# A hybrid decoder block on one core: twelve columns of w_in as split products, both halves of w_out in one wide PSUM tile, mixer outputs normalised ahead of it

## The chip, the cores and the metric

The kernel runs on one core of a Trainium2 chip. The time is what one execution takes on the device, in microseconds; three executions of the kernel before took 1172.45 (the median), 1170.61 and 1172.55 us. All rows below are from one profiled execution of it, which took 1174.26 us; its profiled span is 1172.4 us. Engines: PE multiplies matrices, DVE and POOL do elementwise work, ACT elementwise work with tables (and copies), SP issues most transfers.

## The reference

One layer over 256 positions of width 2048. The mixers take x through w_in (24 columns of 128 channels: 8 for the RG-LRU's input u, 8 for its gate, 8 for the S5 group), each group's result is normalised by itself, and w_out adds it to x; then a gated convolutional FFN of width 6144 follows.

```python
xn = rmsnorm(x, norm1_g[l])
proj = xn @ w_in[l]                       # 2048 -> 3072
rg_u, rg_gate, s5_u = proj[..., :D_RG], proj[..., D_RG:2 * D_RG], proj[..., 2 * D_RG:]
y_rg = rg_lru_group(rg_u, rg_gate, ...)   # conv, gates, linear scan, times gelu(gate)
y_s5 = s5_group(s5_u, ...)                # complex scan over 64 states, out = z * sigmoid(z @ w_glu + b_glu)
mixed = jnp.concatenate([rmsnorm(y_rg, out_norm_rg_g[l]),
                         rmsnorm(y_s5, out_norm_s5_g[l])], axis=-1)
x = x + mixed @ w_out[l]
x = x + conv_gated_mlp(rmsnorm(x, norm2_g[l]), ffn_w_up[l], ffn_conv_w[l], ffn_conv_b[l], ffn_w_down[l])
return rmsnorm(x, final_norm_g)
```

## The kernel before

Activations lie transposed, channels on the 128 partitions and the 256 positions (T) along the row. Weights come as tiles of 128 columns by 8 blocks of 128 rows (512 KB, tile `raw`, four in flight, issued by SP in the order of the program).

There are two kinds of product. `product_whole` (L185) multiplies the raw fp32 weights with fp32 activations, one matmul of 256 columns a block; each shows as two records in the trace. `product` (L170) splits: ACT copies the weights to a high part `wh` (`part`, L150), DVE subtracts it to get the low part `wl` (L151), and the activations have been split in the same way by `split` (high half by ACT, low half by DVE, L202 or L208). A `step` then sums high times high, high times low and low times high: narrow, in three matmuls of 256 columns (L158 to L160), or wide, in one matmul of 512 columns over both halves of the activations (L156) and one of 256 (L160). The wide form leaves two partial sums in PSUM which somebody has to add. Before, only the FFN is wide (`WIDE = "FD"`).

The 24 columns of w_in: four (0, 1, 16, 2) are done in the head while x arrives; the other 20 go through `product_whole`. Weight parts `wh` and `wl` have three buffers each, PSUM has four for products (tag "main") and one each for the small ones of the S5 mixer ("tp", "y", "bu").

The mixers and w_out are written as steps, called in the order of the string `ORDER` (a letter and an index). A scheduler then places the instructions on their engines by its own model of time; on each engine they run in the placed order. The letters: U, P, B and G are the RG-LRU (column of u with its convolution; gates; for four columns at once the decay a4 and the input b4, `rg_batch`; scan and gelu gate, `rg_out`). S, T, K, N, Y and F are the S5 group: its column; tables of sine and cosine, on POOL; matrices, on POOL, with four transposes on PE (L545) whose input `ball` POOL makes (L527), and small matmuls `cb` (L551); N the scan, whose matmuls `bu` (L572) feed a chain on DVE (L577 to L589) that ends in `wx`; Y the matmuls out of `wx` (L599 to L607); gelu. Z splits the S5 results and L multiplies with w_glu, applies the sigmoid and the gate (`s5_glu`). R and Q compute the two groups' 1/rms (`rstd`: a sum by PE, a root by ACT, a reciprocal by DVE, a broadcast by PE, a copy by ACT).

w_out takes one product of 8 blocks for each half of its rows and each of 16 output columns: W the upper half, from the unnormalised RG result. E multiplies W's sum by the group's 1/rms (DVE, L727) and adds it to x (POOL, L728); x is loaded again with the first E. V is the lower half, whose sum DVE multiplies by the other 1/rms and adds to x (L745, L746), then squares and splits for the FFN. That the norm comes after the product is why W and V can't share one PSUM sum.

The stages in the trace: head to 35 us; mixers to 232; W, L, V to about 355; FFN to 1160; final norm.

Of the kernel before, what the change touches and what calls it, by code (L numbers as in the profile page):

```python
# [8 lines left out]
F32 = mybir.dt.float32  # L9
# [5 lines left out]
P = 128  # L15
D = 2048
# [60 lines left out]
def block_kernel(ctx, tc, a, out):  # L77
# [204 lines left out]
    with ExitStack() as ph:
# [387 lines left out]
        def rg_batch(g):  # L670
# [13 lines left out]
            V.tensor_scalar(a4, q4, -2.0, -1.0, ALU.mult, ALU.add)  # L684
            G.tensor_tensor(b4, b4, q4, ALU.mult)
            G.tensor_tensor(b4, b4, tau, ALU.mult)

        def rg_out(j):
# [7 lines left out]
            fn(ge, u, AF.Gelu_apprx_tanh)  # L696
            yv = work.tile([P, T], F32, tag="rg", name="yv")
            V.scalar_tensor_tensor(yv, ge, -1.0, bj, ALU.mult, ALU.mult)
            add_sq(acc_rg, yv, j == 0)
            yr[j] = split(mix, f"y{j}", yv, col("grg", j))  # L700

# [17 lines left out]
        def rg_add(o):  # L719
            if not xr:  # L720
                for i in range(4):
                    t = keep(f"xq{i}", (P, 4, T))
                    nc.sync.dma_start(t, a["xT"][:, 4 * i:4 * i + 4, :])
                    xr.extend(t[:, k, :] for k in range(4))
                    xq2.append(t)
            u = work.tile([P, T], F32, tag="u", name="u")
            V.tensor_tensor(u, total(tops[o], "W" in WIDE), rs["rg"], ALU.mult)  # L727
            G.tensor_tensor(xr[o], xr[o], u, ALU.add)  # L728

        def s5_glu(j):  # L730
            ps = total(product(a["w_glu"], j, (0,), zs, "L" in WIDE), "L" in WIDE)
            sg = work.tile([P, T], F32, tag="cv", name="sg")
            fn(sg, ps, AF.Sigmoid, bias=col("bglu", j))
            ov = work.tile([P, T], F32, tag="rg", name="ov")
# [3 lines left out]
            tag, n = (("wa", WB), ("wb", WB), ("wx", WB), ("bt", WB))[j % 4]  # L738
            ys[j] = split(mw, tag, ov, col("gs5", j), bufs=n)

        def s5_top(o):

            ps = total(product(a["w_out"], o, (1,), ys, "V" in WIDE), "V" in WIDE)
            u = work.tile([P, T], F32, tag="u", name="u")
            V.tensor_tensor(u, ps, rs["s5"], ALU.mult)  # L745
            V.tensor_tensor(xr[o], xr[o], u, ALU.add)  # L746
            add_sq(acc2, xr[o], o == 0)
            x2[o] = split(cpool, f"x{o}", xr[o], col("g2", o))
# [153 lines left out]
```

## Time and profile before

| | before |
|---|---|
| median of three runs | 1172.45 us (1170.61 to 1172.55) |
| the profiled execution | 1174.26 us, span 1172.4 us |
| PE busy | 1145.3 us (98%), mean granted clock 0.988 |
| DVE, ACT, POOL busy | 805.4, 574.3, 209.7 us |

The page gives each engine's busy time, the span in 40 slices of 29.3 us with the busy share in tenths, and the clock granted to PE. A timeline has one row for each run of like instructions: start, time, engine, line, output and inputs, shapes, their count, and in brackets the idle time of the engine ahead with what ended it. Views by line give the count, the sum and the mean of one. PE's records overlap: a step's price is the distance of starts, not the time of a record.

### The profile page before, as it was taken

How to read it: one execution, taken by the hardware profiler on the slowest of the kernel's cores; microseconds unless marked ns; L12 is line 12 of the kernel's file. 1: busy time of each engine (PE TensorE's matmuls, PEld its weight loads, DVE VectorE, ACT ScalarE, POOL GpSimd, SP SyncE). 2: the span in 40 equal slices, each digit the busy share in tenths (PEclk: the TensorE clock that was granted, in tenths of full speed). 3: DMA queues.
4: the chain of work that ended last, by engine and by line, in shares of the span. 5: the costliest groups of instructions: out<-in, count | busy, mean ns of one | idle time of the engine just before them, and what ended most of it. 6: DMA issues, size and time to landing. Idle time of an engine off the chain costs nothing.

```text
span 1172.4 us, 19286 instructions
## 1 busy us (share of the span) xinstructions
PE 1145.3 (98%) x7454; PEld 1014.7 (87%) x7454; DVE 805.4 (69%) x1246; ACT 574.3 (49%) x897; POOL 209.7 (18%) x270
## 2 busy tenths in 40 slices
PE   9998979999999999999999999999999999999996
PEld 8787868889998888888888888888888888888886
DVE  7677564567797777878778787778777444444443
ACT  4342522255466555555555555555555444444432
POOL 5897665124231000000000000000000000000000
PEclk9998989999999999999999999999999999999998
DMA  7434435545566656666656666666656665665662
GB/s 274 139 110 152 134 123 155 170 148 181 180 187 184 187 194 183 195 189 189 195 185 195 186 192 188 190 191 188 193 185 194 183 187 188 183 189 184 186 190 92
DMA packets 65980, 209.27 MB, mean 178 GB/s; under 512 B 11872, under 2 KB 15584, under 8 KB 65888
## 3 DMA queue, kind: packets, MB, share of 16 engines
q1 hardware_dynamic: 65744, 207.97, 56.9%
q8 instruction: 58, 0.95, 0.3%
q14 instruction: 34, 0.28, 0.1%
q10 hardware_dynamic: 144, 0.07, 0.0%
HBM read 204.87 MB, written 2.10 MB: 177 GB/s over the span
## 4 chain that ended last, share of the span: by engine, by line
PE 88%; DVE 4%; POOL 4%; DMA 1%; issue 1%; ACT 1%; SPq 0%; DVEq 0%; ACTq 0%; POOLq 0%
PE ps L156 44%; PE ps L160 27%; PE ps L193 6%; PE ps L159 4%; PE ps L158 4%; PE ps L304 2%; PE y L602 1%; PE y L607 1%; POOL m L525 1%; DMA xq<-in_xT 0%; POOL cp L538 0%; DVE wa L584 0%; POOL m L526 0%; DVE xq L806 0%; POOL tm L506 0%
## 5 line engine op out<-in xcount | busy, mean ns | idle before, releaser
L156 PE MATMUL ps<-sp,wh 128*128 128x512 f32 x2256 | 787.1, 393 | 0.0
L160 PE MATMUL ps<-sp,wl 128*128 128x256 f32 x2624 | 738.0, 281 | 0.0
L151 DVE TENSOR_TENSOR wl<-raw,wh 128x1024 fp32r<-128x1024 f32 x328 | 403.8, 1231 | 245.1 <-ACT wh L150 243.7
L150 ACT CAST wh<-raw 128x1024 fp32r<-128x1024 f32 x328 | 344.8, 1051 | 429.2 <-PE ps L156 251.8
L156 PEld LDWEIGHTS ps<-sp,wh 128*128 128x128 f32 x2256 | 422.6, 187 | 95.6
L160 PEld LDWEIGHTS ps<-sp,wl 128*128 128x128 f32 x2624 | 496.6, 189 | 0.0
L245 POOL TENSOR_TENSOR accx<-accx,sq 128x256 f32<-128x256 f32 x29 | 34.9, 1203 | 800.6 <-ACT sq L244 800.6
L193 PE MATMUL ps<-xg,raw 128*128 128x256 f32 x640 | 146.5, 385 | 0.0
L193 PEld LDWEIGHTS ps<-xg,raw 128*128 128x128 f32 x640 | 121.1, 192 | 17.5 <-issue 0.3
L158 PE MATMUL ps<-sp,wh 128*128 128x256 f32 x368 | 104.6, 285 | 1.9 <-DVE u L727 1.9
L159 PE MATMUL ps<-sp,wh 128*128 128x256 f32 x368 | 104.8, 285 | 0.1
L777 DVE SCALAR_TENSOR_TENSOR cv<-u,par,cv 128x255 f32<-128x255 f32 x192 | 92.3, 480 | 4.1 <-ACT cv L775 0.7
L158 PEld LDWEIGHTS ps<-sp,wh 128*128 128x128 f32 x368 | 71.0, 193 | 2.2 <-DVE u L727 2.0
L159 PEld LDWEIGHTS ps<-sp,wh 128*128 128x128 f32 x368 | 71.1, 193 | 0.4 <-DVE sp L208 0.3
L775 ACT ACTIVATE cv<-u,par 128x256 f32<-128x256 f32 x96 | 57.2, 596 | 0.8 <-DVE u L773 0.8
L773 DVE TENSOR_TENSOR u<-t,rstd 128x256 f32<-128x256 f32 x96 | 40.4, 421 | 1.6
L167 DVE TENSOR_TENSOR t<-t,ps 128x256 f32<-128x256 f32 x96 | 39.7, 414 | 0.0
L166 ACT COPY t<-ps 128x256 f32<-128x256 f32 x96 | 34.7, 361 | 0.0
L304 PE MATMUL ps<-xg,raw 128*128 128x256 f32 x128 | 28.7, 384 | 0.2 <-ACT xg L279 0.2
L304 PEld LDWEIGHTS ps<-xg,raw 128*128 128x128 f32 x128 | 24.5, 193 | 4.0 <-ACT xg L279 0.6
L795 DVE TENSOR_TENSOR xq<-xq,ps 128x256 f32<-128x256 f32 x31 | 13.0, 421 | 16.4 <-PE ps L160 15.9
L538 POOL TENSOR_TENSOR cp<-m,m 64x192 f32<-64x192 f32 x32 | 20.7, 647 | 8.5 <-PE y L607 6.6
(231 smaller groups left out, 697.8 us busy)
## 6 DMA issues: line engine op xcount, KB each, us to landing
raw<-in_w_up SPq DMA_DIRECT2D x192, 512.0 KB, 3.5
raw<-in_w_down SPq DMA_DIRECT2D x96, 512.0 KB, 4.3
raw<-in_w_in SPq DMA_DIRECT2D x47, 512.0 KB, 3.8
raw<-in_w_out SPq DMA_DIRECT2D x32, 512.0 KB, 4.3
raw<-in_w_glu SPq DMA_DIRECT2D x8, 512.0 KB, 3.6
xq<-in_xT SPq DMA_DIRECT2D x7, 512.0 KB, 4.3
out_y<-xq SPq DMA_DIRECT2D x6, 256.0 KB, 2.1
rw<-in_rgw SPq DMA_DIRECT2D x8, 128.0 KB, 3.5
```

What stands on the lines that cost most here:

```text
L150: S.copy(wh, raw)
L151: V.tensor_tensor(wl, raw, wh.bitcast(F32), ALU.subtract)
L156: PE.matmul(ps, lhsT=wh[:, kk, :], rhs=x, start=first, stop=False)
L158: PE.matmul(ps[:, 0, :], lhsT=wh[:, kk, :], rhs=x[:, 0, :], start=first, stop=False)
L159: PE.matmul(ps[:, 0, :], lhsT=wh[:, kk, :], rhs=x[:, 1, :], start=False, stop=False)
L160: PE.matmul(ps[:, 0, :], lhsT=wl[:, kk, :], rhs=x[:, 0, :], start=False, stop=last)
L167: V.tensor_tensor(t, t, ps[:, 0, :], ALU.add)
L193: PE.matmul(ps, lhsT=raw[:, kk, :], rhs=x[j], start=j == 0, stop=j == n - 1)
L304: PE.matmul(ps, lhsT=raw0[i][:, k % KC, :], rhs=xs[k], start=k == 0, stop=k == KX - 1)
L773: V.tensor_tensor(u, ps, rs["n2"], ALU.mult)
L775: S.activation(cv, u, AF.Identity, bias=col("fcb", o), scale=col("fcw", 2 * 2 * KF + o))
L777: V.scalar_tensor_tensor(cv[:, d:], u[:, :T - d], col("fcw", (2 - d) * 2 * KF + o), cv[:, d:], ALU.mult, ALU.add)
```

## The change

Six things change.

1. `WHOLE` names the 12 columns of w_in that stay fp32. The other 12 (U7, S5, S6, S7 and the eight gates) become narrow split products. Their activations are split by the new step A0 (`x_split`), 16 high and 16 low halves in tiles of their own.
2. W and V are wide and go into the same PSUM tile: W opens the sum (`last=False`), V closes it (`first=False`), and DVE adds the two parts to x straight out of PSUM. E is gone, and L is always narrow, as it was.
3. For that the mixer results are normalised first: the new steps H and I (`normed`) multiply by the group's 1/rms on DVE and split. x is loaded again by D0.
4. In `rg_batch` the two products of b4 move from POOL to DVE.
5. The gate's results (`ov`, and the RG result) are written in place of tensors that are done with, no longer into a work tile.
6. `ORDER` is rewritten: Y comes after the next column's N, the S5 steps run further ahead of the columns, all L stand together before W, and V alternates with W from V0 on.

The diff, cut:

```diff
-W0 Z0 Z1 E0 W1 Z2 Z3 E1 W2 Z4 Z5 E2 W3 Z6 Z7 E3 L0 L1 W4 E4 L2 L3 W5 E5 L4 L5 W6 E6 L6 L7 W7 E7 W8 E8 W9 E9 Q0 W10
+Z0 Z1 Z2 Z3 Z4 Z5 Z6 Z7 L0 R0 L1 L2 H0 H1 L3 H2 H3 L4 H4 H5 L5 H6 H7 L6 L7 Q0 W0 W1 W2
+I0 I1 I2 I3 I4 I5 I6 I7 D0 V0 W3 V1 W4 V2 W5 V3 W6 V4 W7 V5 W8 V6 W9 V7 W10 V8 W11 V9 W12 V10 W13 V11 W14 V12 W15
...
+WHOLE = (0, 1, 16, 2, 3, 17, 4, 18, 5, 19, 6, 20)
...
-    WIDE = "FD"
+    WIDE = "FDV"
...
+    def products(ps, src, ot, kcs, xs, wide, first=True, last=True):
...
-                step(ps, wide, wh, wl, kk, xs[j], j == 0, j == n - 1)
+                step(ps, wide, wh, wl, kk, xs[j], first and j == 0, last and j == n - 1)
...
+        def x_split(k):
+            xp.append(split(cpool, f"x{k}", xs[k], None))
+
         def w_in_col(o):
-            return early[o] if o in early else product_whole(a["w_in"], o, (0, 1), xs)
+            if o in early:
+                return early[o]
+            if o in WHOLE:
+                return product_whole(a["w_in"], o, (0, 1), xs)
+            return product(a["w_in"], o, (0, 1), xp)[:, 0, :]
...
-            G.tensor_tensor(b4, b4, q4, ALU.mult)
-            G.tensor_tensor(b4, b4, tau, ALU.mult)
+            V.tensor_tensor(b4, b4, q4, ALU.mult)
+            V.tensor_tensor(b4, b4, tau, ALU.mult)
...
+        def normed(pool, tag, v, r, gcol, **kw):
+            V.tensor_tensor(v, v, r, ALU.mult)
+            return split(pool, tag, v, gcol, **kw)
...
         def rg_top(o):
-            tops[o] = product(a["w_out"], o, (0,), yr, "W" in WIDE)
+            tops[o] = psm.tile([P, 2, T], F32, tag="main", name="ps")
+            products(tops[o], a["w_out"], o, (0,), yr, "V" in WIDE, last=False)
...
-            u = work.tile([P, T], F32, tag="u", name="u")
-            V.tensor_tensor(u, total(tops[o], "W" in WIDE), rs["rg"], ALU.mult)
-            G.tensor_tensor(xr[o], xr[o], u, ALU.add)
...
         def s5_top(o):
-            ps = total(product(a["w_out"], o, (1,), ys, "V" in WIDE), "V" in WIDE)
-            u = work.tile([P, T], F32, tag="u", name="u")
-            V.tensor_tensor(u, ps, rs["s5"], ALU.mult)
-            V.tensor_tensor(xr[o], xr[o], u, ALU.add)
+            products(tops[o], a["w_out"], o, (1,), ys, "V" in WIDE, first=False)
+            flush()
+            for h in range(1 + ("V" in WIDE)):
+                V.tensor_tensor(xr[o], xr[o], tops[o][:, h, :], ALU.add)
```

Three places show what moves. In these rows stand the line, the operation, the output and inputs, the tile's size and a count; lines of the changed kernel are some 3 to 30 higher. The first place is PE between the `cb` matmuls of K0 and those of K1 (`tp` are K1's transposes, `pg` the RG gates). Before:

```order
L551 MATMUL cb<-cp_383,bp_382 32x96 x8
L572 MATMUL bu<-u_520,bt 64x64 x16
L193 MATMUL ps<-xg,raw 128x256 x5
L545 MATMUL tp<-par,ball 128x128 x2
L193 MATMUL ps<-xg,raw 128x256 x3
L545 MATMUL tp<-par,ball 128x128 x2
L193 MATMUL ps<-xg,raw 128x256 x11
```

And in the changed kernel:

```order
L561 MATMUL cb<-cp_383,bp_382 32x96 x8
L582 MATMUL bu<-u_520,bt 64x64 x2
L682 MATMUL pg<-rcv,rw 128x256 x2
L582 MATMUL bu<-u_520,bt 64x64 x14
L555 MATMUL tp<-par,ball 128x128 x4
L200 MATMUL ps<-xg,raw 128x256 x13
```

The eight matmuls of a column that stood between `bu` and the last transposes now stand behind them.

The second place is DVE in the chain of one N late in the mixers, N5 (from `bu` to the last `wx`). Before:

```order
L577 TENSOR_TENSOR wa_1770<-bu_1753,cs_t_1595 128x2x2x128
L577 TENSOR_TENSOR wb_1771<-bu_1753,sn_t_1594 128x2x2x128
L580 TENSOR_TENSOR wa_1770<-wa_1770,wb_1771 128x256
L581 TENSOR_TENSOR wa_1770<-wa_1770,wb_1771 128x256
L584 SCALAR_TENSOR_TENSOR wa_1770<-dec1_393,wa_1770 128x256 x2
L586 TENSOR_TENSOR wx_1772<-wa_1770,cs_t_1595 128x512
L586 TENSOR_TENSOR wb_1771<-wa_1770,sn_t_1594 128x512
L588 TENSOR_TENSOR wx_1772<-wx_1772,wb_1771 128x256
L589 TENSOR_TENSOR wx_1772<-wx_1772,wb_1771 128x256
```

And the second half of such a chain in the changed kernel, from L591 on:

```order
L591 TENSOR_TENSOR wa_1837<-wa_1837,wb_1838 128x256
L154 TENSOR_TENSOR wl_2061<-raw_2058,wh_2060 128x1024
L710 SCALAR_TENSOR_TENSOR xq1_420<-xq3_418,xq1_420 128x256 x4
L594 SCALAR_TENSOR_TENSOR wa_1837<-dec1_393,wa_1837 128x256 x2
L712 TENSOR_TENSOR u_1981<-ps_1919,rstd1_233 128x256
L154 TENSOR_TENSOR wl_2192<-raw_2189,wh_2191 128x1024
L596 TENSOR_TENSOR wx_1839<-wa_1837,cs_t_1581 128x512
L596 TENSOR_TENSOR wb_1838<-wa_1837,sn_t_1580 128x512
L715 SCALAR_TENSOR_TENSOR xq0_419<-ge_1983,xq0_419 128x256
L154 TENSOR_TENSOR wl_2222<-raw_2219,wh_2221 128x1024
L598 TENSOR_TENSOR wx_1839<-wx_1839,wb_1838 128x256
L599 TENSOR_TENSOR wx_1839<-wx_1839,wb_1838 128x256
```

The nine rows of the chain stood together; now three low parts of split columns (`wl`), four scans (L710) and two steps of the gates stand inside it.

The third place is DVE around Q0, behind the reciprocal of the S5 norm. Before, `u` (L727) is the product of one W, which nothing of V waits for:

```order
L220 RECIPROCAL rs<-rs 128x2
L727 TENSOR_TENSOR u<-ps,rstd_rg 128x256
L151 TENSOR_TENSOR wl<-raw,wh 128x1024
L727 TENSOR_TENSOR u<-ps,rstd_rg 128x256
L151 TENSOR_TENSOR wl<-raw,wh 128x1024
```

And in the changed kernel, where L733 are the multiplications of I and L215 the low halves of V's activations:

```order
L227 RECIPROCAL rs<-rs 128x2
L154 TENSOR_TENSOR wl<-raw,wh 128x1024
L733 TENSOR_TENSOR xq_417<-xq_417,rstd_s_3084 128x256 x4
L733 TENSOR_TENSOR xq_418<-xq_418,rstd_s_3084 128x256 x4
L215 SCALAR_TENSOR_TENSOR sp<-xq_417,par,sp 128x256 x4
L215 SCALAR_TENSOR_TENSOR sp<-xq_418,par,sp 128x256 x4
```

Eight multiplications now stand between the norm and the first half that V0 reads.

## Rows read from the trace of the kernel before

**Rows 1.** The page: busy time by engine; POOL's busy tenths in 40 slices.

```profile
PE 1145.3 (98%) x7454; PEld 1014.7 (87%) x7454; DVE 805.4 (69%) x1246; ACT 574.3 (49%) x897; POOL 209.7 (18%) x270
...
POOL 5897665124231000000000000000000000000000
```

**Rows 2.** Timeline of PE, whole fp32 columns: start, us, engine, line, operation.

```profile
180.68 14.51 PE L193 MATMUL ps<-xg,raw 128*128 128x256 f32 x66
195.12 0.69 PE L572 MATMUL bu<-u,bt 64*64 64x64 f32 x32
```

**Rows 3.** Timeline of PE, steps of split products, narrow and wide.

```profile
262.24 0.28 PE L158 MATMUL ps<-sp,wh 128*128 128x256 f32 x1
...
262.60 0.28 PE L158 MATMUL ps<-sp,wh 128*128 128x256 f32 x1
...
499.82 0.39 PE L156 MATMUL ps<-sp,wh 128*128 128x512 f32 x1
...
501.90 0.39 PE L156 MATMUL ps<-sp,wh 128*128 128x512 f32 x1
```

**Rows 4.** Timeline of PE, three waits; in brackets idle time and releaser.

```profile
100.24 0.65 PE L599 MATMUL y<-wx,cp 128*32 128x64 f32 x16 [3.24 <-ACT ig L119]
...
154.81 0.44 PE L599 MATMUL y<-wx,cp 128*32 128x64 f32 x8 [6.67 <-DVE wx L588]
...
249.50 0.58 PE L158 MATMUL ps<-sp,wh 128*128 128x256 f32 x1 [1.86 <-DVE u L727]
```

**Rows 5.** Windows of PE: length, busy (records), granted clock, DMA share, GB/s.

```profile
105.00:106.00 1.00, 1.00 (x4) 0.50 0.87 311
```

**Rows 6.** PE's waits on POOL: us in total, times, the longest.

```profile
PE tp L545 <- POOL ball L527: 2.2, 3, 0.8
...
PE cb L551 <- POOL cp L538: 1.1, 1, 1.1
```

**Rows 7.** Timelines of PE and POOL around K1's transposes.

```profile
58.35 2.42 PE L193 MATMUL ps<-xg,raw 128*128 128x256 f32 x10
...
62.95 0.44 PE L545 MATMUL tp<-par,ball 128*128 128x128 f32 x2 [0.66 <-POOL ball L527]
...
61.90 1.00 POOL L527 TENSOR_TENSOR ball<-m,m 128x256 f32<-128x256 f32 x1
```

**Rows 8.** DVE by line, 40 to 110 us: count, busy us, mean ns, idle.

```profile
L577 DVE TENSOR_TENSOR wa<-bu,cs_t 128x512 f32<-128x512 f32 x3 | 2.1, 692 | 3.5 <-PE bu L572 3.5
...
L589 DVE TENSOR_TENSOR wx<-wx,wb 128x256 f32<-128x256 f32 x2 | 1.7, 826 | 0.0
```

**Rows 9.** DVE by line, 205 to 236 us.

```profile
L151 DVE TENSOR_TENSOR wl<-raw,wh 128x1024 fp32r<-128x1024 f32 x3 | 3.6, 1217 | 3.7 <-ACT wh L150 3.7
...
L577 DVE TENSOR_TENSOR wa<-bu,cs_t 128x512 f32<-128x512 f32 x2 | 1.4, 684 | 0.0
...
L589 DVE TENSOR_TENSOR wx<-wx,wb 128x256 f32<-128x256 f32 x1 | 0.4, 418 | 0.0
```

**Rows 10.** DVE by line, 110 to 231 us.

```profile
L577 DVE TENSOR_TENSOR wa<-bu,cs_t 128x512 f32<-128x512 f32 x5 | 3.4, 687 | 1.4 <-PE bu L572 1.3
...
L589 DVE TENSOR_TENSOR wx<-wx,wb 128x256 f32<-128x256 f32 x5 | 3.3, 651 | 0.0
```

**Rows 11.** Timelines of ACT, POOL and PE: one gate's chain, then Q0's norm.

```profile
262.72 1.05 ACT L150 CAST wh<-raw 128x1024 fp32r<-128x1024 f32 x1 [1.11 <-issue]
263.68 0.47 ACT L119 ACTIVATE sg<-ps,par 128x256 f32<-128x256 f32 x1
...
267.47 1.03 POOL L245 TENSOR_TENSOR acc_s<-acc_s,sq 128x256 f32<-128x256 f32 x1 [4.56 <-ACT sq L244]
...
291.40 0.50 PE L216 MATMUL ss<-ones,acc_s 128*128 128x1 f32 x4
...
292.59 1.28 ACT L119 ACT_TABLE_LOAD   x1
...
297.04 0.37 ACT L227 COPY rstd_s<-rb 128x256 f32<-128x256 f32 x1 [1.19 <-PE rb L223]
```

More of the change, by code (lines that the diff above doesn't have):

```diff
@@ L172, in product @@
         ps = psm.tile([P, 2, T], F32, tag="main", name="ps")
+        products(ps, src, ot, kcs, xs, wide)
+        flush()
+        return ps
+    def products(ps, src, ot, kcs, xs, wide, first=True, last=True):
         n = len(kcs) * KC
@@ L272, in x_scale @@
         if k % 2 == 0:
-            pair = cpool.tile([P, 2, T], F32, tag=f"x{KH + k // 2}", name="xg")
+            if k < KX - 2:
+                pair = cpool.tile([P, 2, T], F32, tag=f"x{KH + k // 2}", name="xg")
+            else:
+                pair = mix.tile([P, 2, T], F32, tag="y7", name="xg")
             xs.extend((pair[:, 0, :], pair[:, 1, :]))
@@ L696, in rg_out @@
             fn(ge, u, AF.Gelu_apprx_tanh)
[L697 to L700, printed above, removed]
+            V.scalar_tensor_tensor(bj, ge, -1.0, bj, ALU.mult, ALU.mult)
+            add_sq(acc_rg, bj, j == 0)
         def s5_u(c):
@@ L713, in s5_split, with rg_normed, s5_normed, x_again @@
             zs[c] = split(cpool, f"x{c}", us[c].rearrange("p b t -> p (b t)"), None)
-        def rg_top(o):
-            tops[o] = product(a["w_out"], o, (0,), yr, "W" in WIDE)
[L719 to L725, printed above, removed]
-            u = work.tile([P, T], F32, tag="u", name="u")
-            V.tensor_tensor(u, total(tops[o], "W" in WIDE), rs["rg"], ALU.mult)
-            G.tensor_tensor(xr[o], xr[o], u, ALU.add)
+        def normed(pool, tag, v, r, gcol, **kw):
+            V.tensor_tensor(v, v, r, ALU.mult)
+            return split(pool, tag, v, gcol, **kw)
+        def rg_normed(j):
+            yr[j] = normed(mix, f"y{j}", bu[j // 4][:, j % 4, :], rs["rg"], col("grg", j))
+        def s5_normed(j):
+            ys[j] = normed(mw, ("wa", "wb", "wx", "bt")[j % 4], aa[j // 4][:, j % 4, :], rs["s5"], col("gs5", j), bufs=WB)
+        def x_again():
+            for i in range(4):
+                t = keep(f"xq{i}", (P, 4, T))
+                nc.sync.dma_start(t, a["xT"][:, 4 * i:4 * i + 4, :])
+                xr.extend(t[:, k, :] for k in range(4))
+                xq2.append(t)
+        def rg_top(o):
+            tops[o] = psm.tile([P, 2, T], F32, tag="main", name="ps")
+            products(tops[o], a["w_out"], o, (0,), yr, "V" in WIDE, last=False)
         def s5_glu(j):
-            ps = total(product(a["w_glu"], j, (0,), zs, "L" in WIDE), "L" in WIDE)
+            ps = product(a["w_glu"], j, (0,), zs)[:, 0, :]
             sg = work.tile([P, T], F32, tag="cv", name="sg")
             fn(sg, ps, AF.Sigmoid, bias=col("bglu", j))
-            ov = work.tile([P, T], F32, tag="rg", name="ov")
+            ov = aa[j // 4][:, j % 4, :]
             V.tensor_tensor(ov.rearrange("p (t b) -> p b t", b=BL), us[j],
@@ L737, in s5_glu @@
             add_sq(acc_s5, ov, j == 0)
[L738 to L739 removed]
         def s5_top(o):
[L743 to L746 removed]
+            products(tops[o], a["w_out"], o, (1,), ys, "V" in WIDE, first=False)
+            flush()
+            for h in range(1 + ("V" in WIDE)):
+                V.tensor_tensor(xr[o], xr[o], tops[o][:, h, :], ALU.add)
             add_sq(acc2, xr[o], o == 0)
@@ L756, in block_kernel @@
             "Y": lambda c: s5_out(c, outs[c], *mats[c][3:]),
-            "W": rg_top, "E": rg_add, "V": s5_top,
+            "W": rg_top, "V": s5_top, "A": lambda _: [x_split(k) for k in range(KX)],
+            "H": rg_normed, "I": s5_normed, "D": lambda _: x_again(),
             "R": lambda _: rs.update(rg=rstd([acc_rg], DH, "rstd_rg")),
```

10 lines of the change are left out of this document (4 added, 6 removed).

## The prediction, made before the changed kernel ran

> **What bounds the kernel now.** I read first the page's table of busy time: TensorE (PE) works 98% of a span of 1172.4 us, DVE 69%, POOL 18% [rows 1]. So the time is PE's work plus the idle time of PE, and a change pays by taking matmul time out, and costs by what it makes PE wait for. Next, the timeline of PE gives the price of each kind of product. A plain fp32 column of w_in: 66 records, two for each matmul, run from 180.68 to 195.12 us, 33 matmuls in 14.44 us, 0.438 us each [rows 2]. A step of a split product in three narrow matmuls begins every 0.36 us (262.24, 262.60), and a wide step in two every 0.347 us (six from 499.82 to 501.90) [rows 3]. Last, the waits and the clock of PE. In the stage of the mixers PE lost: 3.24 us up to 100.24, and then half clock (granted 0.50, which is 1.2 GHz in place of 2.4) until about 106, 5.8 us in which half is lost, 2.9 us; 6.67 and 0.21 us up to 155.46 with 2.8 us of the same kind behind; 1.86 us up to 249.50 with 0.33 ahead of it and 1.5 us of slow clock [rows 4, 5]; and at K0 and K1 2.2 and 1.1 us for POOL [rows 6]. That is 6.1 + 9.7 + 3.7 + 3.3 = **22.8 us** of loss, nearly all in the first 255 us. From there to the end PE runs on.
>
> **What the change takes from PE.** Twelve of the 24 columns of w_in become split products: 16 steps each, 16 x 0.438 = 7.00 us before, 16 x 0.36 = 5.76 us after, 1.24 us less, 12 x 1.24 = **14.9 us**. All 32 products of w_out become wide, 256 steps x 0.013 = **3.3 us** [rows 2, 3]. This is work of the engine that is never off, so it counts whole: -18.2 us, if no wait grows.
>
> **What it adds elsewhere, at nothing.** The pair W, V costs DVE two low parts (2 x 1.22), two adds out of PSUM (2 x 0.42) and the low half of x2 (0.42 to 0.83, as L589), 4.1 us at most, beside 2 x 8 x 0.347 = 5.56 us of PE [rows 3, 8, 9]: hidden; without the E steps it is less than before. If that cover were gone, each pair would add its difference. The normalising mults of the RG half (H, 8 x 0.42) lie among the L products, where DVE has 2.88 us for each 1.22 us of low part and about 1 us of gate: hidden. The reload of x (D0) is queued on SP behind three weight tiles of w_out and ahead of the next eight; the weights are four tiles ahead, so nobody waits. The first V needs W4's place in PSUM and two adds, 0.7 us; I count it. The split of x puts 9 casts on ACT and 9 subtractions of 0.42 us on DVE into the head, among the small instructions that make the S5 constants. It can push POOL's start on K0 by 0 to 3 us, into the wait that comes next.
>
> **K0 and K1.** PE does the transposes of K1 in its own order. Before, eight whole matmuls (3.5 us) lay between K0's bu and K1's last two transposes; still it waited 0.66 us, since the second half of ball left POOL only at 61.90 + 1.00 = 62.9 us [rows 7]. The new order puts all four transposes right behind bu and two pg matmuls, which end at about 59.3. POOL's chain is the same, so the wait there is about 3.6 us in place of 0.66, and 6.2 in place of 3.3 for K0 and K1. A wait of 3.24 us was followed by half clock [rows 4, 5], so 2.9 us more: **9.1 us**, between 3.3 (POOL earlier) and 12 (the head pushed by 3).
>
> **The split columns.** Here a resource that was free becomes tight. Each split column asks two low parts of DVE, 2 x 1.22 = 2.4 us in 5.76 [rows 9], beside the chains of N, and the two mults of b4 (1024 wide, 1.22 like a low part) now stand on DVE too. DVE is in order: y for S5 waits for wx, and wx stands behind low parts, b4 and scans. From the first split column's low part to the wx of N5 there are 79 instructions on DVE: 14 low parts 17.2, three N chains 17.3, the 7 wide ones of a batch 7.0 (0.7 to 1.23 each), and 28 small ones 13.2, **54.7 us** at the durations of 205 to 236 us, where POOL was nearly idle. At those of 40 to 110, where POOL was 8 to 9 tenths busy [rows 1], the same rows sum to 77.7, because instructions with two inputs in SBUF stretch: L589 takes 418 ns there and 826 here, while L577, with one input in PSUM, takes 684 and 692 [rows 8, 9]. PE's work up to the matmuls that want that wx is 46.4 us by the prices above, and DVE can be three low parts ahead (3.7). So PE is late by 54.7 - 46.4 - 3.7 = 4.6 us with a quiet POOL and by 27.6 with a loaded one. Which? From 110 to 231 us the nine rows of a chain summed to 6.9 us, against 5.8 quiet and 8.5 loaded (first and last of them in each window are L577 and L589) [rows 8, 9, 10], four tenths of the way, with POOL 5 to 6 tenths busy for most of it [rows 1]. POOL now loses the wide products of b4, so I take a little less, 0.35 of the way: 54.7 + 8.1 = 62.8, PE late by **12.7 us**, plus one drop of the clock, 2.9. For the y of the first three columns, ahead of these, I take 1 us (0 to 6): the waits of 3.24 and 6.67 themselves should go, as Y now comes a whole N later.
>
> The Trainium skill, SBUF — State Buffer, section Who interferes with whom, says that a DVE instruction with two inputs in SBUF contends with one of GpSimd that reads SBUF, and that of the pair in contention one blocks for the whole instruction. L589 and L577 agree with it; by its sharp form the split phase would cost the loaded end, which is the third rival below.
>
> **Q0.** All L now come first, and only W0 to W3 (32 steps, 11.1 us) lie between L7's last matmul and V0, since PSUM holds four. Before, six whole W lay there. On PE's row stand W0 to W2 (24 steps, 8.3 us), the sum for the norm, W3, the broadcast, V0. The gate's chain is over by then: a cast of ACT in the way (1.05), then sigmoid, gate, square and POOL's add, 263.68 to 268.50, make 5.9 us. From the sum on: 1.2 us to the load of ACT's table (291.40 to 292.59), 1.28 for it, about 0.5 for root and reciprocal (an estimate; small ones), so the reciprocal is there at 8.3 + 3.0 = 11.3 us, and W3 hides it up to 8.3 + 0.5 + 2.8 = 11.6. The broadcast (0.6) ends at 12.2. Then the copy, 0.37 behind another cast of 1.05: 13.6 [rows 11]; eight mults in a row on DVE, 0.42 each: 17.0; the first high and low half, 0.4 each: 17.8 [rows 9]. PE idles from 12.2 to 17.8, 5.6 us, and then runs 5.8 us at half clock: **8.5 us**, between 4.6 (no cast in the way, clock kept) and 9.7 (a low part of 1.2 ahead of the mults).
>
> **The sum.** Losses after: 9.1 + 1 + 12.7 + 2.9 + 8.5 + 0.7 = 34.9 us, 12.1 more than 22.8. Net -18.2 + 12.1 = -6.1 us. The profiled execution took 1174.26 us, 1.8 above the median of the three runs, 1172.45; against its own time 1168.2, on the median's scale **1166 us**.
>
> **Rivals.** (1) POOL does not slow DVE where it matters: the split phase loses 4.6 with no drop of the clock, y nothing. 9.1 + 4.6 + 8.5 + 0.7 = 22.9, no more than now, and the whole 18.2 is kept: 1154 us. For it: low parts kept 1.22 near the end of the mixers. Against: the chains from 110 to 231 were not at their quiet price. (2) The gains and the waits cancel: losses of 39 to 43 us, 1170 to 1175 us. (3) **Slower**: DVE beside POOL. With 0.6 of the way to the loaded durations DVE needs 68.5 us, PE is late by 18.4, each of two waits drops the clock (5.8), and the earlier y wait 6: 9.1 + 6 + 18.4 + 5.8 + 8.5 + 0.7 = 48.5, 25.7 more than now; 1172.45 - 18.2 + 25.7 = 1180 us. For it: from 40 to 110 us everything with two inputs in SBUF ran loaded [rows 8]. Against: POOL has less to do after. It decides from the point where the split phase and y with their clock cost 22.7 us (41.0 in all eats the 18.2): 0.6 of the way with one drop and 1 us for y, 0.3 with two and the full 6.
>
> **How the numbers follow.** Forecast (1158 to 1170): 0.45. Rival 1 (1147 to 1158): 0.23. Rival 2 (1170 to 1175): 0.10. Rival 3 (1175 to 1190): 0.22. Within 0.2%, 1170.1 to 1174.8, is about what a measurement can't tell from no change: 0.10. Faster 0.68, slower 0.22. The range that leaves out a tenth on each side is 1150 to 1180.
>
> **What would show it.** Right: the split columns at 0.36 us a step, V with W at 0.347; idle of PE ahead of y in the split phase with DVE's wx as releaser; a wait of some 3.6 us for ball at K1; one of 5 to 6 us ahead of V0, released by DVE's low half, half clock behind it. Wrong: no wait at V0 (then ACT and DVE got through earlier than their order tells); L589 at 0.42 all through the split phase (rival 1) or above 0.7 (rival 3); a wait in the head for the casts of x.

## The result and the profile after

The changed kernel took 1185.37 us in the median of nine runs, against 1172.45 before: a ratio of 1.0082, 95% interval 1.0064 to 1.0101, so it is slower, by 0.8%. The nine times lie in two groups with nothing between them, three from 1174.56 to 1177.22 and six from 1185.34 to 1186.76; the kernel before has one group (1170.61 to 1175.58). The profiled execution at hand is of the lower group: 1177.22 us, span 1175.4, mean granted clock 0.985.

The page of the changed kernel, the lines that answer to [rows 1]:

```profile
PE 1135.8 (97%) x7390; PEld 1000.8 (85%) x7390; DVE 839.2 (71%) x1290; ACT 603.7 (51%) x938; POOL 207.7 (18%) x250
...
POOL 5799874131221000000000000000000000000000
```

PE has less work and is idle more. What it waited for (us in total, times, the longest):

```profile
PE y L609 <- DVE wx L598: 6.0, 3, 3.1
PE tp L555 <- POOL ball L537: 5.1, 4, 2.2
PE ps L159 <- DVE sp L215: 4.9, 1, 4.9
PE ps L163 <- DVE wl L154: 3.8, 3, 1.7
PE cb L561 <- POOL cp L548: 2.8, 3, 1.3
```

The timeline at the places that the prediction spoke of: the first row is POOL's, K0's work; the others are PE's, K1's last transposes, the first y inside the split columns, and V0.

```profile
45.90 1.12 POOL L535 TENSOR_TENSOR m<-pk,fr 128x256 f32<-128x256 f32 x1 [2.48 <-DVE fr L471]
...
64.87 0.44 PE L555 MATMUL tp<-par,ball 128*128 128x128 f32 x2 [2.22 <-POOL ball L537]
...
137.01 0.32 PE L609 MATMUL y<-wx,cp 128*32 128x64 f32 x8 [3.15 <-DVE wx L598]
...
277.42 0.80 PE L159 MATMUL ps<-sp,wh 128*128 128x512 f32 x1 [4.91 <-DVE sp L215]
```

Each of these waits is where it was expected, released by the engine named. The stretch 160 to 190 us, first of the changed kernel, then of the one before (length, then busy time and records of PE, PEld, DVE, ACT and POOL, then granted clock, DMA share, GB/s):

```profile
160.00:190.00 30.00, 24.69 (x299) 21.92 (x299) 30.00 (x36) 14.35 (x26) 21.32 (x20) 0.86 0.43 128
```

```profile
160.00:190.00 30.00, 29.89 (x240) 25.33 (x239) 15.37 (x24) 8.00 (x23) 20.08 (x29) 0.99 0.49 144
```

DVE goes from half busy to 30.00 of 30 us, PE from full to 24.69 at a clock of 0.86. DVE by line from 120 to 192 us, to be held against [rows 8 to 10]:

```profile
L154 DVE TENSOR_TENSOR wl<-raw,wh 128x1024 fp32r<-128x1024 f32 x14 | 20.2, 1446 | 3.6 <-ACT wh L153 3.6
...
L587 DVE TENSOR_TENSOR wa<-bu,cs_t 128x512 f32<-128x512 f32 x4 | 2.7, 680 | 0.1
...
L599 DVE TENSOR_TENSOR wx<-wx,wb 128x256 f32<-128x256 f32 x3 | 2.2, 734 | 0.0
```

**The pace of a wide step.** W and V run at 0.353 us a step (six from 299.62 to 301.74), FFN's up products at 0.347 (four from 599.88 to 601.27 make 1.39):

```profile
299.62 0.40 PE L159 MATMUL ps<-sp,wh 128*128 128x512 f32 x1
...
301.74 0.40 PE L159 MATMUL ps<-sp,wh 128*128 128x512 f32 x1
...
599.88 0.39 PE L159 MATMUL ps<-sp,wh 128*128 128x512 f32 x1
...
601.27 0.39 PE L159 MATMUL ps<-sp,wh 128*128 128x512 f32 x1
...
368.42 0.61 PE L230 MATMUL rb<-par,rs 128*128 128x128 f32 x4
...
1165.98 0.71 PE L230 MATMUL rb<-par,rs 128*128 128x128 f32 x4 [0.55 <-DVE rs L227]
```

The last two rows enclose FFN, from the norm ahead of it to the final norm: 797.6 us, and 797.6 before (365.44 to 1162.99). In the lower group, then, all that changed lies ahead of 368 us.

### The profile page after: what moved, and what is told of

The parts are those of the page before. It is cut to its first block, busy times and chain, and to the rows that moved or that the text cites. A ratio compares the mean times of both kernels' runs of the same rounds, so it can differ in the third digit from the quotient of the medians.

```text
span 1175.4 us, 19237 instructions
## 1 busy us (share of the span) xinstructions
PE 1135.8 (97%) x7390; PEld 1000.8 (85%) x7390; DVE 839.2 (71%) x1290; ACT 603.7 (51%) x938; POOL 207.7 (18%) x250
## 4 chain that ended last, share of the span: by engine, by line
PE 85%; DVE 7%; POOL 4%; issue 1%; ACT 1%; DMA 1%; SPq 0%; DVEq 0%; ACTq 0%; POOLq 0%
PE ps L159 49%; PE ps L163 28%; PE ps L161 2%; PE ps L162 2%; PE ps L200 2%; DVE wl L154 1%; POOL cp L548 1%; PE y L612 1%; DVE sp L209 1%; PE y L617 1%; DMA xq<-in_xT 1%; DVE xq L829 0%; DVE rcv L668 0%; ACT wh L153 0%; POOL ball L537 0%
## 5 line engine op out<-in xcount | busy, mean ns | idle before, releaser
L159 PE MATMUL ps<-sp,wh 128*128 128x512 f32 x2512 | 879.4, 394 | 5.4 <-DVE sp L215 4.9
L163 PE MATMUL ps<-sp,wl 128*128 128x256 f32 x2816 | 793.5, 282 | 3.8 <-DVE wl L154 3.8
L154 DVE TENSOR_TENSOR wl<-raw,wh 128x1024 fp32r<-128x1024 f32 x352 | 435.2, 1236 | 256.8 <-ACT wh L153 253.7
L153 ACT CAST wh<-raw 128x1024 fp32r<-128x1024 f32 x352 | 369.6, 1051 | 439.7 <-PE ps L159 282.8
L159 PEld LDWEIGHTS ps<-sp,wh 128*128 128x128 f32 x2512 | 471.3, 188 | 113.6 <-DVE sp L215 5.1
L163 PEld LDWEIGHTS ps<-sp,wl 128*128 128x128 f32 x2816 | 533.9, 190 | 5.3 <-DVE wl L154 4.6
L161 PE MATMUL ps<-sp,wh 128*128 128x256 f32 x304 | 87.9, 290 | 0.0
L162 PE MATMUL ps<-sp,wh 128*128 128x256 f32 x304 | 87.3, 287 | 0.0
L200 PE MATMUL ps<-xg,raw 128*128 128x256 f32 x256 | 60.5, 390 | 0.0
L161 PEld LDWEIGHTS ps<-sp,wh 128*128 128x128 f32 x304 | 59.4, 196 | 0.7 <-issue 0.3
L162 PEld LDWEIGHTS ps<-sp,wh 128*128 128x128 f32 x304 | 59.4, 195 | 0.3 <-issue 0.2
L200 PEld LDWEIGHTS ps<-xg,raw 128*128 128x128 f32 x256 | 48.8, 194 | 7.4
L314 PE MATMUL ps<-xg,raw 128*128 128x256 f32 x128 | 28.3, 380 | 1.7 <-ACT xg L289 0.9
L314 PEld LDWEIGHTS ps<-xg,raw 128*128 128x128 f32 x128 | 24.1, 190 | 5.6 <-ACT xg L289 2.3
L548 POOL TENSOR_TENSOR cp<-m,m 64x192 f32<-64x192 f32 x32 | 23.8, 744 | 7.6 <-PE y L617 5.8
```

The source lines that it names most:

```text
L153: S.copy(wh, raw)
L154: V.tensor_tensor(wl, raw, wh.bitcast(F32), ALU.subtract)
L159: PE.matmul(ps, lhsT=wh[:, kk, :], rhs=x, start=first, stop=False)
L161: PE.matmul(ps[:, 0, :], lhsT=wh[:, kk, :], rhs=x[:, 0, :], start=first, stop=False)
L162: PE.matmul(ps[:, 0, :], lhsT=wh[:, kk, :], rhs=x[:, 1, :], start=False, stop=False)
L163: PE.matmul(ps[:, 0, :], lhsT=wl[:, kk, :], rhs=x[:, 0, :], start=False, stop=last)
```

## The experiments

Times are medians of kernels timed together with the kernel before, ratios are to it, with 95% intervals. A loss is PE's idle time plus what a granted clock below 1 took from its busy time, summed over windows of 1 us; up to the sum of the FFN's norm it was 24.4 us before and 41.8 in the changed kernel's profiled execution.

**Where do the two groups differ?** `a0` is the changed kernel once more.

> The changed kernel as it is, once more. Its nine times lay in two groups, 1174.6 to 1177.2 and 1185.3 to 1186.8 us; the trace at hand is of the lower group. Theory A (DVE and POOL in each other's way in the stretch of the split columns): both groups show again, some 9 us apart, and where a trace of the upper group comes out, the extra 9 us are idle and half-clock time of PE between 120 and 200 us, ahead of y, with DVE's wx or wl as releaser. Theory B (something that has nothing to do with the split columns, a transfer or PE's clock later on): the extra time lies behind 240 us or is spread.

Five runs: 1173.82, 1176.81, 1185.93, 1186.21, 1186.74. The profile is of the upper group, and theory A had the place of the extra time wrong: up to the norm this execution is as quick as the one of the lower group (its norm's broadcast stands at 367.37 us, the other's at 368.42), and FFN takes 807.6 us instead of 797.6. From PE's timeline, the enclosing rows of FFN and five steps inside it:

```profile
367.37 0.61 PE L230 MATMUL rb<-par,rs 128*128 128x128 f32 x4
...
599.72 0.40 PE L159 MATMUL ps<-sp,wh 128*128 128x512 f32 x1
...
601.48 0.40 PE L159 MATMUL ps<-sp,wh 128*128 128x512 f32 x1
...
1174.97 0.71 PE L230 MATMUL rb<-par,rs 128*128 128x128 f32 x4 [0.55 <-DVE rs L227]
```

1.76 us for five steps, 0.352; over longer stretches 0.353, from the first up product to the last, no idle time, granted clock 1.00. FFN's up stage has 96 x 16 = 1536 wide steps; 1536 x 0.0066 = 10.1 us is the whole gap. (The down stage runs at 0.353 in every kernel here, the one before included.) The profiled executions of the upper group that follow (`allwhole`, `b4pool`, `second`) have FFN at 807.6 us too.

Three more kernels, each the changed one with one part undone; the diffs are cut.

```diff
 # allwhole: all of w_in whole, A0 taken out of ORDER
+WHOLE = tuple(range(24))
 # b4pool
-            V.tensor_tensor(b4, b4, q4, ALU.mult)
+            G.tensor_tensor(b4, b4, q4, ALU.mult)     # and the second likewise
 # narrow
-    WIDE = "FDV"
+    WIDE = "FD"
```

> The changed kernel with all 24 columns of w_in whole (no split of x, no low parts for them), everything else as changed. PE's work grows by 12 x 1.24 = 14.9 us. Theory A: the waits and half clock between 120 and 200 us (18.4 us in the trace at hand) fall to some 5 us and the two groups of times become one: 1172 to 1178 us, so that the split columns gave nothing. Theory B: the waits of that stretch stay, 1187 us or more, and the two groups stay.

> The changed kernel with the two products of b4 on POOL again. Theory A in the form that DVE's row is what is full: each batch takes 2 x 1.2 to 1.6 us off DVE, PE's losses between 120 and 200 us fall by 2 to 5 us: 1172 to 1184 us. In the form that POOL is what is full: POOL gets 2 x 5 us, T and K come later, 3 to 10 us slower. Theory B: no change.

> The changed kernel with W and V narrow (three matmuls a step, one PSUM sum, one add), everything else as changed. By the steps in FFN (0.347 against 0.360) 256 steps cost 3.3 us more; by the steps of W and V in the trace of the changed kernel (0.353 from 299.62 to 301.74) 1.8 us. No change of the two groups.

`allwhole`: 1175.62 to 1178.81 in four runs, 1185.99 to 1188.10 in three. So the split columns don't make the groups; and its lower group is that of the changed kernel or a little above it, so they bring little or nothing. In its profile the loss from 120 to 200 us is 6.5 us, as theory A had it, against 18.4 in the changed kernel's. `b4pool`: 1180.01 and 1182.78, 1189.99 and 1190.04: some 5.5 us slower in the lower group and 4 in the upper, as the form with a full POOL has it. `narrow`: eight runs from 1174.90 to 1177.46, one group, 1.0028 (1.0018 to 1.0038). The expectation (both groups, 1.8 to 3.3 us slower) was wrong in the main point: without wide products of w_out the upper group is gone.

**What sets FFN's pace?**

```diff
 # second: the kernel before up to F7, b4 on POOL, all whole, then the changed order from Z0 on
 # lastnarrow
-            products(tops[o], a["w_out"], o, (1,), ys, "V" in WIDE, first=False)
+            products(tops[o], a["w_out"], o, (1,), ys, o < KX - 1, first=False)    # W and the adds likewise
 # firstnarrow
+            wide = o not in (0, KF)
+            ps = total(product(a["w_up"], o, (0, 1), x2, wide), wide)
 # lastadd: lastnarrow, and
+            if o == KX - 1:
+                V.scalar_tensor_tensor(xr[o], tops[o][:, 0, :], 0.0, xr[o], ALU.mult, ALU.add)
```

> The mixers of the kernel before (its order, b4 on POOL, all 24 columns whole) with the second half of the changed one (all L, normalised results, W and V wide in one PSUM tile). Theory C, from the runs so far: the two groups differ only in FFN's up products, whose step takes 0.347 us in one and 0.353 in the other, and the slow pace appears only where wide products of w_out stand ahead of FFN. Then this kernel has both groups, 10 us apart. The lower one: the second half loses some 7.5 us (L and Q0) in place of 3.7 and saves 1.8: about 1174 to 1176; the upper one 1184 to 1186. Theory A (the split columns make the groups): one group at 1174.

> The changed kernel with the last pair of w_out alone (W15 and V15) narrow. Theory C in the form that FFN inherits the pace of the products right ahead of it: one group only, 1174 to 1178 us, as with all of w_out narrow. In the form that anything wide earlier in the program is enough, or that chance decides: both groups, 1176 and 1186.

> The changed kernel with FFN's first two up products (columns 0 and 48, 16 steps each) narrow, w_out wide. Theory C, first form (the pace of the up products is set by the form of what PE ran just ahead of the norm's small matmuls): one group, 1175 to 1178 us. Second form (it is V's wide products or their two adds that leave the state, whatever follows): both groups, 1176 and 1186.

> The kernel whose last pair of w_out alone is narrow (one group, 1175.6 us), with one more DVE pass of 256 columns on the last x, of the kind and size of the second add that a wide pair has (it adds zero times the sum). PE's program is as with the narrow last pair, DVE's time at the end of w_out as with the wide one. If the two groups come from DVE's timing at the hand-over to FFN: both groups are back, 1176 and 1186. If they come from PE's own sequence: one group, 1175 to 1177.

`second`: 1182.73 and 1182.77, 1193.48 and 1194.09; both groups with no split column and the old mixers, as theory C has it. The level was missed by 7 to 9 us: the old mixers' end and the new second half fit badly, PE waits for low parts of L, 2.94 us at the most:

```profile
258.57 0.39 PE L163 MATMUL ps<-sp,wl 128*128 128x256 f32 x1 [2.94 <-DVE wl L154]
```

`lastnarrow`: ten runs from 1174.32 to 1176.67, 1.0022 (1.0013 to 1.0031): one narrow pair out of sixteen and the upper group is gone. `lastadd`: ten from 1174.13 to 1176.03: DVE's extra pass at the hand-over doesn't bring it back. `firstnarrow`: four runs, 1184.83 to 1186.80, all upper. So a narrow product ahead of the norm doesn't help as such, and the first form of theory C fell. Over all kernels here the upper group came in 16 of the 29 runs in which the last pair of w_out and all of FFN's up products were wide, and in none with the last pair narrow: the last pair does decide whether it can come. In the profiles of `firstnarrow` and `lastadd` W and V ran at 0.3475, and FFN's up stage at 0.353 in the one and 0.347 in the other: the pace of one stage doesn't foretell the next.

Can small matmuls change the pace? Two kernels on the base of the one before, `poke_before` and `downnarrow`, put small fp32 products inside down products (`downnarrow` with a narrow first one). The diff is cut: `like_sum` and `like_rb` are two small matmuls each, called between the two matmuls of the step counted.

```diff
+            for n, f in {1: [(24, like_sum)], 2: [(24, like_rb)], 4: [(16, like_sum), (12, like_rb)],
+                         6: [(12, like_rb), (12, like_rb)]}.get(o, []):
+                poke.append([n, lambda f=f, v=xr[o - 1]: f(v)])
             ps = product(a["w_down"], o, range(KF // KC), hs, wide)
 # downnarrow
-            wide = "D" in WIDE and o < KX - 1
+            wide = "D" in WIDE and 0 < o < KX - 1
```

> The kernel before with six small fp32 products of 128 columns or of one put between the two matmuls of a step in FFN's down products (in columns 1, 2, 4 and 6; their results are not used). Theory C: the pace of wide steps is a state that small matmuls between them can change, as at the norm ahead of FFN; the down products, at 0.353 in all kernels so far, fall to 0.347 behind some of the six and keep it: up to 14 x 48 steps x 0.0066 = 4.4 us less, 1168 us. Rival E: the pace belongs to the operands of a stage (tiles, places in memory) and no small matmul changes it: 0.353 to the end, 1174 us (the six cost about 2 us).

> The kernel before with the six small products in the down stage (1175.8 us, down at 0.353) and the first down product narrow, 48 steps. Theory C, first form: behind a narrow product the small ones bring the step to 0.347 and it stays: 14 x 48 x 0.0066 = 4.4 us less and 0.6 more, 1171 to 1173 us. Theory E (the down stage has its pace from its operands): 0.353, 1176 to 1177 us.

`poke_before`: 1175.78 us (1.0029, 1.0016 to 1.0041); `downnarrow`: 1175.67 us (1.0020, 1.0009 to 1.0031). The down steps keep 0.353 behind all six places in both. Theory E held for the down stage, but E can't be all: the up stage has the same operands in both groups.

**Where does the pace turn?** The traces show more than the means. In the up stage of every slow trace the steps aren't evenly slow: the distances of their starts come in a rhythm of three, about 0.350, 0.361 and 0.349 us, where all quick steps are 0.347. And where FFN's steps turn quick, they do so at the small matmuls of the norm ahead of it, `ss` (the sum) and `rb` (the broadcast), which stand inside FFN's first two up products. What comes of them goes with the place in the rhythm at which `ss` falls. The last four wide steps ahead of `ss`, first in the changed kernel's lower group, then in `a0`, then in `lastnarrow`:

```profile
362.80 0.40 PE L159 MATMUL ps<-sp,wh 128*128 128x512 f32 x1
...
363.15 0.40 PE L159 MATMUL ps<-sp,wh 128*128 128x512 f32 x1
...
363.50 0.40 PE L159 MATMUL ps<-sp,wh 128*128 128x512 f32 x1
...
363.86 0.40 PE L159 MATMUL ps<-sp,wh 128*128 128x512 f32 x1
364.10 0.50 PE L223 MATMUL ss<-ones,accx 128*128 128x1 f32 x4
```

```profile
361.74 0.40 PE L159 MATMUL ps<-sp,wh 128*128 128x512 f32 x1
...
362.10 0.40 PE L159 MATMUL ps<-sp,wh 128*128 128x512 f32 x1
...
362.45 0.40 PE L159 MATMUL ps<-sp,wh 128*128 128x512 f32 x1
...
362.80 0.40 PE L159 MATMUL ps<-sp,wh 128*128 128x512 f32 x1
363.04 0.50 PE L223 MATMUL ss<-ones,accx 128*128 128x1 f32 x4
```

```profile
361.72 0.40 PE L159 MATMUL ps<-sp,wh 128*128 128x512 f32 x1
...
362.07 0.40 PE L159 MATMUL ps<-sp,wh 128*128 128x512 f32 x1
...
362.43 0.40 PE L159 MATMUL ps<-sp,wh 128*128 128x512 f32 x1
...
362.78 0.40 PE L159 MATMUL ps<-sp,wh 128*128 128x512 f32 x1
363.01 0.50 PE L223 MATMUL ss<-ones,accx 128*128 128x1 f32 x4
```

The long step (0.36) is the last, the first and the second of the three distances. In `lastnarrow` the steps are quick from `ss` on, and the 13 other traces with a narrow last pair (the kernel before among them) are like it. In `a0` neither `ss` nor `rb` changes the rhythm, and the three other slow traces with a wide last pair (`allwhole`, `b4pool`, `second`) are like it. The changed kernel's lower group is alone: slow up to `rb`, quick behind it. In `firstnarrow` there is no wide step ahead of `ss`, and behind its narrow ones the wide ones begin slow, as FFN's first up product does in the kernel before. With a narrow last pair the rhythm begins anew with FFN's first product, 15 steps ahead of `ss`; with a wide one it runs on from W and V, and can meet `ss` at another place in each run. This is read from one trace of each kernel. No run moves `ss` or `rb` by a step, so it is not shown that the place is the cause.

**Why do the split columns bring nothing?**

```diff
 # narrow_whole: narrow, and all of w_in whole
 # split_old: the kernel before with x_split, w_in_col and product as in the change, and
+WHOLE = (0, 1, 16, 2, 3, 17, 4, 18, 5, 6, 19, 7)
 # nolow: narrow, and for w_in
+            if src is a["w_in"]:
+                wl = wh                                  # no subtraction either
 # lightpool: narrow, and
-            for m, (x1, x2_, op) in enumerate(((cr4, ci4, ALU.subtract), (ci4, cr4, ALU.add))):
+            for m, (x1, x2_, op) in enumerate((...) if c < 3 else ()):
```

> The changed kernel with all columns whole and w_out narrow: of the change only the order, the normalising ahead of w_out and b4 on DVE are left; PE's work is that of the kernel before. Against the kernel with narrow w_out (1176.5) this undoes the split columns without the two groups in the way. Theory A (split columns cost in waits what they save in matmuls, 12.7 to 14.9 us): 1172 to 1178 us, no more than 3 us from 1176.5. If the split columns keep their gain: 1186 us or more. One group.

> The kernel before with 12 split columns and nothing else of the change (the columns G0 to G7 and S4 to S7, the split of x behind U7). PE's work falls by 12.7 to 14.9 us. Theory A (DVE's low parts beside its N chains): DVE fills up in the stretch of the split columns here too, waits and half clock grow by 5 to 15 us: 1160 to 1174 us. A rival, that the new order makes the waits and not the split columns: 1158 to 1161 us. One group.

> The changed kernel with w_out narrow (1176.5 us, one group), and without the low parts of the split columns: their third matmul uses the high part again, so this product leaves the correction by the low parts out. PE's work is the same; DVE is free of 24 low parts, some 32 us, in the stretch of the split columns. Theory A (DVE's row is full there): PE's waits on wx and wl between 120 and 200 us and the half clock behind them (19 us of loss with w_out narrow) fall by 8 to 14 us: 1162 to 1169 us. Rival D (POOL's chain of T and K paces the stretch, DVE only follows): less than 4 us.

> The changed kernel with w_out narrow (1176.5 us), and with K's C matrices made for the first three S5 columns only (the later five use what lies in their tiles, so this leaves a part of the computation out): POOL is free of some 25 us of work, PE's and DVE's instructions are the same. Rival D: POOL's waits at cb and tp behind 60 us (some 5 us) and most of the loss between 120 and 200 us go, 1160 to 1168 us. Theory A with DVE's row as the limit: DVE gains only by contention, a few us (some 0.3 us for each instruction that no longer meets POOL): 1170 to 1175 us.

`narrow_whole`: 1176.07 us, 1.0029 (1.0018 to 1.0040), `narrow`: 1176.5, 1.0028. `split_old`: 1172.80 us, 1.0001 (0.9991 to 1.0010). Twelve split columns are worth nothing with the new order and nothing with the old. Up to the norm's sum `narrow` has 12.9 us less work on PE than `narrow_whole` and 13.7 us more loss. `nolow`: 1165.74 us, 10.8 less than `narrow`, inside theory A's range. `lightpool`: 1168.83 us, 7.7 less, between rival D's range (0.8 above it) and theory A's. Neither engine alone is the cause. From 120 to 200 us, `narrow`, `nolow` and `lightpool` in this order, columns as above:

```profile
120.00:200.00 80.00, 69.81 (x814) 63.58 (x816) 73.34 (x95) 41.25 (x77) 58.28 (x63) 0.91 0.44 130
```

```profile
120.00:200.00 80.00, 74.39 (x955) 68.97 (x954) 56.06 (x85) 45.59 (x86) 48.14 (x62) 0.98 0.47 149
```

```profile
120.00:200.00 80.00, 73.69 (x946) 68.13 (x945) 69.19 (x97) 44.27 (x85) 32.15 (x31) 0.98 0.47 145
```

Taking 24 low parts off DVE makes POOL's busy time fall too (58.28 us for 63 instructions to 48.14 for 62), and taking work off POOL makes the same low part cheaper on DVE, 1458 ns in `narrow` and 1326 in `lightpool`:

```profile
L154 DVE TENSOR_TENSOR wl<-raw,wh 128x1024 fp32r<-128x1024 f32 x17 | 24.8, 1458 | 5.2 <-ACT wh L153 5.2
```

```profile
L154 DVE TENSOR_TENSOR wl<-raw,wh 128x1024 fp32r<-128x1024 f32 x18 | 23.9, 1326 | 7.4 <-ACT wh L153 7.4
```

Each holds the other up, and both stand in the chain from `bu` to y. The rule of the Trainium skill, SBUF — State Buffer, section Who interferes with whom, that a DVE instruction with two inputs in SBUF contends with one of GpSimd that reads SBUF, agrees: the low part has both its inputs there, and L587, with an input in PSUM, kept 680 ns.

**How many, and where?** On the kernel before, the last 4 columns split, then the last 7; then the two products of b4 on DVE, with the 7 and alone.

```diff
 # split_few, x_split behind S6
+WHOLE = tuple(c for c in range(24) if c not in (13, 14, 23, 15))
 # split_seven, x_split behind S5
+WHOLE = tuple(c for c in range(24) if c not in (11, 12, 22, 13, 14, 23, 15))
 # seven_b4 (on split_seven), b4_alone (on the kernel before)
-            G.tensor_tensor(b4, b4, q4, ALU.mult)
+            V.tensor_tensor(b4, b4, q4, ALU.mult)     # and the second likewise
```

> The kernel before with 4 split columns only (G5, G6, S7, G7, the last ones, where POOL is nearly idle and DVE busy 52% of the time), the split of x behind S6. PE's work falls by 4 x 1.1 to 1.24 = 4.4 to 5 us. Theory A (a split column costs what it meets on DVE and POOL): here it meets little, the split of x itself (16 x 0.42 to 0.9 us on DVE) apart: 1168 to 1171 us. Rival: a split column gives nothing wherever it stands: 1172 to 1173.

> The kernel before with 7 split columns (G3, G4, S6, G5, G6, S7, G7; the split of x behind S5). PE's work falls by 7 x 1.1 to 1.24 = 7.7 to 8.7 us. With 4 the time fell by 2.6 us, with 12 by nothing. Theory A (a split column costs what it meets on DVE and POOL; ahead of 205 us POOL is 5 to 6 tenths busy): the three further ones bring nothing or cost, 1170 to 1172 us. Rival: only the split of x is a fixed cost and each column gives 1.2: 1166 to 1167 us.

> The kernel before with 7 split columns (1168.5 us) and the products of b4 on DVE. In the changed kernel, where 12 columns are split, putting b4 back on POOL cost some 4 to 5 us in the lower group. Theory A with POOL's chain in it (a product of 1024 columns takes POOL 2.4 to 2.8 us and blocks DVE the while, DVE 1.2): 2 to 5 us less, 1163 to 1167 us. Rival (DVE is the fuller of the two here): no gain, 1168 to 1171 us.

> The kernel before with the products of b4 on DVE and nothing else changed. DVE is no more than 64% busy between 120 and 200 us here. Theory A with POOL's chain: 1 to 4 us less, 1169 to 1172 us, the wait of 6.7 us ahead of y at 154.8 us shorter. Rival: no change or slower, 1172 to 1175 us.

`split_few`: 1170.10 us, 0.9974 (0.9965 to 0.9984). `split_seven`: 1168.47 us, 0.9957 (0.9941 to 0.9973). `b4_alone`: 1169.93 us, 0.9978 (0.9967 to 0.9988), so this part of the change is a gain by itself. In its profile the loss from 120 to 200 us falls from 9.8 to 4.1 us, as expected, and from 80 to 120 us it rises from 6.2 to 9.4. `seven_b4`: 1169.97 us, 0.9972 (0.9962 to 0.9983): the two don't add up, as the rival had it. `split_seven` lies between the two ranges expected of it, 1.5 us from either: the gain is still there with seven columns, counted from the end, and gone with twelve. How much the three behind the fourth add is not settled, since the two intervals overlap. `split_seven` beats both kernels.

## Why the prediction was wrong

**The step that failed** is the sentence that ends its first part: from the first 255 us to the end PE runs on. It took the wide step as one price, 0.347 us, from FFN, and put a change of FFN's time at nothing. The same two instructions take 0.347 or 0.353, for a whole stage. That cost 10 us in FFN, in six runs of nine, and it put the median above the range. The rows at hand showed only the quick pace; FFN's down steps and its first up product, had they been read too, run at 0.353 in the kernel before, and the prediction gave no room to it. The same step mis-sized the gain of w_out: 256 x (0.360 - 0.353) = 1.8 us, not 3.3; in the timing, `narrow` against `lastnarrow`, 0.9, which is not clear of noise (1.0028 and 1.0022, with overlapping intervals).

**The rest, against the lower group.** This group lies above the forecast too (1174.56 to 1177.22, against 1158 to 1170). The forecast on the profiled execution's own scale was 1168.2; it took 1177.2. Of the 9 us, 2.0 are the work of the split columns (12.9 us saved, not 14.9; a step does take 0.36, and where the difference lies was not found), 1.5 the pace of W and V, and the rest losses, 17.4 us more than before where 12.1 were expected:

| | expected | measured in the lower group |
|---|---|---|
| head (0 to 40 us) | in K0's | 3.1, before 1.2 |
| K0, K1 (40 to 80) | 9.1 | 8.2 |
| first y (80 to 120) | 1 | 3.0, most of it for POOL, none ahead of y; before 6.2 |
| split columns (120 to 200) | 12.7 + 2.9 | 9.4 idle + 9.0 clock, before 9.8 |
| L behind Z (240 to 260) | 0 | 2.3 |
| Q0, V0 | 8.5 + 0.7 | 6.8 |

K0 and K1: right in place, and in size in part by luck. The single wait was 2.22 us and not 3.6, PE's waits for POOL 5.3 and not 6.2, the clock 1.7 and not 2.9, and 1.2 us of a wait for DVE (`rcv`), which wasn't in the sum, made up for some of it; POOL starts K0 at 45.90, 2.2 us later than before, so the split of x did push it as far as the range had it (POOL starts at 45.8 to 46.8 in all traces with split columns, at 43.7 to 44.6 in those without). The split columns: right place, releasers and mechanism, DVE late beside POOL; the mis-sized part is the clock. It fell to half three times and not once: behind the wait of 3.15 us at 137.01, behind two of 0.88 and 0.55 at 163 to 164, and behind one of 1.66 at 184.67, where it stayed low past a further wait of 1.98. A wait of that size doesn't always bring it: `narrow` has two of 0.86 and 0.55 us at the same place and kept the full clock. The windows there, the changed kernel first (columns as above):

```profile
164.60:168.00 3.40, 3.40 (x74) 3.11 (x73) 3.40 (x4) 1.29 (x3) 2.28 (x2) 0.50 0.36 133
```

```profile
163.50:168.00 4.50, 3.95 (x101) 3.47 (x100) 4.50 (x4) 2.20 (x6) 4.27 (x5) 1.00 0.50 149
```

The nine rows of a chain of N summed to 7.3 us from 120 to 200 us, 0.57 of the way from 5.8 to the loaded 8.5 and not 0.35; L599 alone was at 0.73 us, past the 0.7 that was named as the sign of the third rival. The third rival had this mechanism (it is worked out at 0.6 of the way, not at the loaded end, with the clock falling twice); its point of decision, 22.7 us for the stretch with y, was not reached (18.4), and the lower group is slower than before only with the head, L and the smaller gains. Q0: the chain was as worked out, 4.91 us idle against 5.6, with 1.5 us of clock against 2.9. The low parts of L, behind eight low halves of Z on DVE, were not in the sum at all.

**The parts by themselves.** Order, normalising first and b4 on DVE together: +3.4 us (`narrow_whole` 1176.07 against 1172.65). Split columns: +0.4, and all of w_out but the last pair wide: -0.9, neither clear of noise. The last pair wide: nothing in three runs of nine, 10 us in six.

**What stays open** is why a stage has one pace or the other. Shown: it is not idle time, not the granted clock, not the operands alone (same tiles, both paces); the last pair of w_out decides whether the slow one can come, and then chance; DVE's extra pass has no part in it, and small matmuls in the down stage don't change it. Read from the traces and not tested: the place in the rhythm of three at which the norm's small matmuls fall. Why such a rhythm exists was not found.

## What to carry to other kernels

Read the price of a repeated instruction in every stage in which it occurs, and in more than one execution: 7 ns in 350, over 1500 steps, weighed more here than the net of all the rest of the change (10 us against some 3.5). A change that trades PE's time for another engine's is limited by the stretch in which it lands, so apply it there by the piece, from the end with the most room, and stop where it stops to pay. Where two engines slow each other, add up the row at its quiet and at its loaded durations and look for what lies between (here 0.57 of the way), and give the clock's drop a place in the range for each group of waits, not for one: here it fell three times in 80 us, once behind waits of 0.88 and 0.55 us.

## What the runs showed of the hardware

A wide step (512 columns, then 256) has two paces, 0.3467 and 0.353 us, kept for 500 us at a time at a granted clock of 1.00, and one program can take either from run to run. The quick one is even; the slow one is a mean of three steps in turn, 0.350, 0.361 and 0.349 us in FFN's up stage. Small fp32 products dropped between its matmuls cost about 3 us for six places and left the pace as it was.
